# Encoder layer on one core: first norm, its products and the first weight pieces in another order

## The chip, the cores and the metric
The program runs on 1 core of one Trainium2 chip. Its engines are TensorE (PE, with its weight loads PEld), VectorE (DVE), ScalarE (ACT), GpSimd (POOL) and SyncE (SP, which here only issues transfers). The metric is the device time of one execution in microseconds (us). Three runs of the kernel before took 1007.52, 1008.33 and 1009.56 us; the median is 1008.33 us.

## The reference, cut to what matters
One post-norm layer on 512 tokens of 1024 features, all in float32. The part that the change touches is the first norm and the first products of the input projection:

```python
h = layer_norm(x, ln0_g, ln0_b)            # x: (1, 512, 1024)
proj = h @ w_in[l] + b_in[l]               # w_in: (1024, 9728)
...                                        # short convolution, dilated attention, gates
h = layer_norm(ALPHA * h + mix, ln1_g[l], ln1_b[l])
...                                        # gated MLP
h = layer_norm(ALPHA * h + ffn, ln2_g[l], ln2_b[l])
```

## The kernel before, in words
Every matrix product of float32 accuracy is made of three products of rounded operands. A weight or activation is split into a high part (`hi`, a rounded copy made on ACT) and a low part (`lo`, the rest, a subtraction); `mm3` (L312) then adds hi*hi, hi*lo and lo*hi into one PSUM tile. Here m = 0, 1, 2 names these three.

The weights come as one stream of pieces of 128 x 2048 ("chunks"; chunk 0 holds the blocks n = 0 and 1 of the input projection, chunk 1 the blocks n = 2 and 3, chunk 2 the next two). `load` (L241) issues a chunk's transfer on SP into one of only two raw buffers; `split` (L250) makes hi on ACT and lo on POOL for chunks 0 and 1, on DVE for the rest; `chunk` (L268) splits the chunk that is needed and the next, and loads the one after. A raw buffer is free once its lo is made, and the transfer of a later chunk waits on SP for that.

The first norm goes by two halves hf of two token tiles of 128 tokens (x0, x1, then x2, x3). For each half DVE computes the statistics (`bn_half`, L276), `ln_finish` (L282) makes 1/sqrt with a square root on ACT (L288) and a few tiny DVE operations, and DVE normalises x in place (L304). PE transposes x to feature-major (L345, with the identity in `cols`), ACT scales it out of PSUM (`lnT`, L308), DVE makes the high part (L309) and the low part (L310) of the eight tiles hT0 to hT7. Then PE does 96 products of 256 token columns: four blocks n, eight k, three m. The 40 bfloat16 products on `warm` (L229) at the start feed nothing. `kbd`, two tiles for the keys, are set to zero by DVE (L226).

Each engine runs its queue strictly in the order in which the instructions stand. The order is made by a scheduling layer that may move instructions of independent steps past each other; `tc.issue_after(ins)` keeps the instructions of a block that are on the engine of `ins` behind it, and `tc.keep_in_program_order` keeps marked instructions in the order of the program. The layer also decides which of the two raw buffers a new chunk gets: the one that it sees free first.

Of the kernel before, what the change touches and what calls it, by code (L numbers as in the profile page):

```python
# [11 lines left out]
P = 128  # L12
D = 1024
T = 512
KT = D // P
# [6 lines left out]
MASKED = -1e33  # L22
WARM = 40

# order of the rows of per-feature vectors that are broadcast over partitions
ROWS = ("ln0_g", "ln0_b", "b_o", "ln1_g", "ln1_b", "b_down", "ln2_g", "ln2_b")
# columns of the per-partition parameter table
C_ID = 0
# [19 lines left out]
def in_units():  # L48
    """Blocks of 128 columns of w_in in the order of their use."""
    units = []  # L50
    for p in range(NPAIR):
        for g in range(3):
            for kind, base in (("q", BLK_Q), ("k", BLK_K), ("v", BLK_V)):
                units.append((kind, p, g, base + g * 4 + p))
    for j in range(8):
        units += [("C", j, 0, BLK_C + j), ("H", j, 0, BLK_H + j), ("B", j, 0, BLK_B + j)]
    return units


def chunk_plan():  # L60
    """(name, columns) of each piece of the weight stream, in the order of its use."""
    out = [("in", i, 2048) for i in range(0, len(in_units()), 2)]
    out += [("wa", j, 2048) for j in range(0, 8, 2)]
    for j0 in (0, 4):
        out.append(("wb", j0, 2048))
        out += [("gate", j, 2048) for j in range(j0, j0 + 4)]
    for half in range(2):
        for kh in range(2):
            out.append(("wo", (half, kh), 2048))
    for part in range(2):  # L70
        for j in range(part * FFH, (part + 1) * FFH):
            out.append(("up", j, 2048))
        for half in range(2):
            for c, n in ((0, 4), (4, 4), (8, 3)):
                out.append(("dn", (part, half, c, n), n * 512))
    return out


def lay_out_weights(w):
    """The weights as one stream of [128, columns] pieces; only moves elements."""  # L80
    w_in, w_a, w_b, w_o = w["w_in"][0], w["w_a"][0], w["w_b"][0], w["w_o"][0]
# [53 lines left out]
def distance_tables():  # L135
    """-(distance) of query (partition) and key (column), MASKED where not attended to."""
    q = np.arange(P)[:, None]
# [9 lines left out]
def build(tc, x, wst, colt, dist, rows, out):  # L147
# [3 lines left out]
    with ExitStack() as ctx:  # L151
# [34 lines left out]

# [1 line left out]
        xr = x.rearrange("(i r) d -> r i d", r=4)  # L188
# [16 lines left out]

        first_load(xt[0], xr[0])
        first_load(xt[1], xr[1])
        first_raw(0, 0)
# [13 lines left out]
        nc.vector.memset(warm, 0.0)  # L222
        # keys of a pair of heads, block diagonal: rows of head h are zero outside of [:, h]
        kbd = [blk(F32R, (2, 512), f"kbd{n}") for n in range(2)]
        for t in kbd:
            nc.vector.memset(f(t), 0.0)  # L226
        wps = ps("u")
# [7 lines left out]

# [1 line left out]
        plan = chunk_plan()  # L237
# [12 lines left out]
        def split(i):  # L250
# [8 lines left out]
            for c in starts:  # L259
                part = slice(c, min(c + step, n))  # L260
                nc.scalar.activation(hi[:, part], raws[i][:, part], AF.Copy)  # L261
                eng = nc.gpsimd if i < 2 else nc.vector
                eng.tensor_tensor(lo[:, part], raws[i][:, part], f(hi[:, part]), op=ALU.subtract)  # L263
            splits[i] = (hi, lo)

        where = {(c[0], c[1]): i for i, c in enumerate(plan)}
# [7 lines left out]

# [1 line left out]
        def bn_half(st, z, h):  # L276
            nc.vector.bn_stats(out=st[:, h, :], in_=z[:, h * 512 : (h + 1) * 512])

# [3 lines left out]
        def ln_finish(sts_, name):  # L282
            n = len(sts_)
            mv = small.tile([P, 8, n], F32, tag=f"mv{n}", name=name + "mv", bufs=4)
            for i, st in enumerate(sts_):
                nc.vector.bn_aggr(out=mv[:, 0:2, i], in_=st.rearrange("p a b -> p (a b)"))
            # 1/sqrt(v): the square root's table, then one Newton step
            roots.append(nc.scalar.activation(mv[:, 2], mv[:, 1], AF.Sqrt, bias=eps).ins)  # L288
# [14 lines left out]
        def normalise(z, mean, rstd):  # L303
            nc.vector.tensor_scalar(z, z, mean, rstd, op0=ALU.subtract, op1=ALU.mult)  # L304

        def feature_major(pst, dst, kt, cg, cb, c0, c1):
            t = f32t("lnT")[:, : c1 - c0]
            nc.scalar.activation(t, pst, AF.Identity, bias=col(cb + kt), scale=col(cg + kt))  # L308
            nc.vector.tensor_copy(dst[:, 0, c0:c1], t)  # L309
            nc.vector.tensor_tensor(dst[:, 1, c0:c1], t, f(dst[:, 0, c0:c1]), op=ALU.subtract)  # L310

# [5 lines left out]
        def unit(o, w, c0, rhs, t0=0, t1=512):  # L317
            """o[128 features, tokens] = the block of weights at column c0, times rhs."""
            n = len(rhs)
# [3 lines left out]

# [1 line left out]
        stats0 = []  # L325
        hT = [blk(F32R, (2, 512), f"hT{k}") for k in range(KT)]
        first = []
        for hf in range(2):
            rr = (2 * hf, 2 * hf + 1)
            st = [bn_tile(f"l0{r}") for r in rr]  # L330
            for i, r in enumerate(rr):
                for h in range(2):
                    bn_half(st[i], xt[r], h)
            stats0 += ln_finish(st, f"l0{hf}")
            for r in rr:
                normalise(xt[r], *stats0[r])
            if hf == 0:
                with tc.issue_after(roots[0]):
                    chunk("in", 0)
            for k0 in range(0, KT, 2):  # L340
                pst = ps(("pt", "s")[k0 // 2 % 2])
                for k in (k0, k0 + 1):
# [3 lines left out]
                for k in (k0, k0 + 1):  # L346
                    c = (k % 2) * 256
                    feature_major(pst[:, c : c + 256], hT[k], k, C_G0, C_B0, hf * 256, hf * 256 + 256)
            if hf == 0:
                first = [ps("acc"), ps("acc"), ps("u"), ps("u")]  # L350
            t = slice(hf * 256, hf * 256 + 256)
            for n0, nk in ((0, [(n, k) for k in range(KT) for n in range(2)]), (2, [(n, k) for n in range(2) for k in range(KT)])):
                w = chunk("in", n0)
                for n, k in nk:
                    a = slice(n * 1024 + k * P, n * 1024 + (k + 1) * P)
                    mm3(first[n0 + n][:, t], w[0][:, a], w[1][:, a], hT[k][:, 0, t], hT[k][:, 1, t], k == 0, k == KT - 1)

# [4 lines left out]
        def nat(ap):  # L362
            """Token columns in the order (r, i) as seen in a tile whose columns are tokens 4i + r."""
            return ap.rearrange("p (i r) -> p r i", r=4)
# [3 lines left out]

# [1 line left out]
        sl = slopes()  # L370
# [42 lines left out]
        class Job:  # L413
            """Two heads times 512 columns of scores: a query tile and its window of 256 keys
            (group 0), or two residue classes of 128 queries and as many keys."""

# [68 lines left out]
            def c(self):  # L485
                """Adds to the sums over keys; rows of one head are of use in its own columns."""
                p, g, n = self.key
# [37 lines left out]
        def merge(p):  # L525
            """Weights of the groups' unnormalised outputs: exp(m_g - m) over the sum of all."""
            st1, st2 = sts[p, 1], sts[p, 2]
# [26 lines left out]

# [36 lines left out]

# [1 line left out]
        vtodo, late, scores, sums, scaled, running = [], [], [], [], [], []  # L593
# [52 lines left out]

# [1 line left out]
        ya = []  # L648
        for j in range(8):
# [55 lines left out]

# [1 line left out]
        def tok_mm(o, act, w, kts, r, k0, first, last, f0=0, f1=512):  # L707
# [28 lines left out]
        for r in range(4):  # L736
# [21 lines left out]

# [1 line left out]
        g2 = b2 = None  # L760
# [79 lines left out]
```

## Time and profile before
| What | Value |
|---|---|
| median of three runs | 1008.33 us |
| span of the profiled execution, first to last instruction | 1004.4 us |
| TensorE busy | 974.7 us, 97% of the span |
| VectorE / ScalarE / GpSimd busy | 551.0 / 398.2 / 70.2 us |
| mean granted TensorE clock | 0.985 of full speed |

The page gives no time of the profiled execution apart from its span; the 3.9 us between the span and the median of the runs lie before the first and behind the last instruction and are taken as the same for both kernels. TensorE bounds the program: after the first 15 us it hardly stops. What is read here is therefore the start, up to the last product of the first four blocks at about 41 us, and what ends each wait there.

### The profile page before, as it was taken

To read this page: it belongs to the slowest core of one execution; us is meant where nothing else is said; L and a number is where in the kernel's file an instruction comes from. 1 tells how busy PE (TensorE), PEld (TensorE's weight loads), DVE (VectorE), ACT (ScalarE), POOL (GpSimd) and SP (SyncE) were. 2 spreads that over 40 slices of the span, in tenths; PEclk is the share of its full clock that TensorE was granted. 3 is DMA by queue.
4 is the path that set the end of the run, shared out by engine and by line. 5 is a ranking of instruction groups with operands and counts; after the bars stand their busy time and mean duration, and the time that the engine had idled before them with its cause. 6 is when DMAs were issued, how large, how long until landed. Compare 5 with 4: busy or idle time off the path is not lost.

```text
span 1004.4 us, 11766 instructions
## 1 busy us (share of the span) xinstructions
PE 974.7 (97%) x4729; PEld 821.6 (82%) x4729; DVE 551.0 (55%) x863; ACT 398.2 (40%) x679; POOL 70.2 (7%) x161
## 2 busy tenths in 40 slices
PE   7999999999999999999999997799999999999996
PEld 7988888888888888888888886688888888888885
DVE  7856658657675445322355769664542345445256
ACT  4655564564543333233343223254442234444220
POOL 4000000000000000000000304400000000000000
PEclk9999999999999999999999997799999999999998
DMA  6322322122322212225243420232232322321402
GB/s 231 127 87 85 83 81 70 58 85 84 85 85 85 84 59 110 84 84 206 87 138 110 171 84 6 80 126 84 87 112 74 107 103 89 121 84 73 157 1 84
DMA packets 23462, 96.74 MB, mean 96 GB/s; under 512 B 9200, under 2 KB 9584, under 8 KB 13680
## 3 DMA queue, kind: packets, MB, share of 16 engines
q1 hardware_dynamic: 14256, 89.60, 25.6%
q0 software_dynamic: 1728, 6.29, 1.8%
q10 hardware_dynamic: 7424, 0.10, 0.4%
q8 instruction: 37, 0.61, 0.3%
q14 instruction: 17, 0.14, 0.0%
HBM read 93.84 MB, written 2.15 MB: 96 GB/s over the span
## 4 chain that ended last, share of the span: by engine, by line
PE 86%; DVE 8%; DMA 2%; ACT 2%; issue 1%; ACTq 0%; DVEq 0%
PE ps_acc L313 15%; PE ps_acc L314 15%; PE ps_acc L315 15%; PE ps_s L313 5%; PE ps_s L315 5%; PE ps_s L314 5%; PE ps_u L313 5%; PE ps_u L314 5%; PE ps_u L315 5%; PE ps_pt L313 4%; PE ps_pt L315 4%; PE ps_pt L314 4%; DMA s<-st 1%; DVE h1T L310 1%; PE ps_pt L479 1%; DVE h1T L309 1%
## 5 line engine op out<-in xcount | busy, mean ns | idle before, releaser
L263 DVE TENSOR_TENSOR lo<-raw,hi 128x1024 fp32r<-128x1024 f32 (+1 forms) x160 | 190.6, 1211 | 185.1 <-ACT hi L261 183.5
L261 ACT ACTIVATE hi<-raw 128x1024 fp32r<-128x1024 f32 (+1 forms) x166 | 166.6, 1033 | 231.0 <-PE ps_acc L314 67.5
L313 PE MATMUL ps_acc<-hT,hi 128*128 128x512 f32 (+1 forms) x512 | 198.6, 388 | 1.2 <-DVE kbd L392 0.9
L314 PE MATMUL ps_acc<-hT,hi 128*128 128x512 f32 (+1 forms) x512 | 196.7, 384 | 0.1
L315 PE MATMUL ps_acc<-hT,lo 128*128 128x512 f32 (+1 forms) x512 | 196.5, 384 | 0.0
L313 PEld LDWEIGHTS ps_acc<-hT,hi 128*128 128x128 f32 x512 | 96.5, 189 | 20.4 <-PE ps_pt L479 1.6
L315 PEld LDWEIGHTS ps_acc<-hT,lo 128*128 128x128 f32 x512 | 96.4, 188 | 19.2
L314 PEld LDWEIGHTS ps_acc<-hT,hi 128*128 128x128 f32 x512 | 96.5, 189 | 17.7 <-DVE hT L310 0.3
L460 ACT ACTIVATE S<-S,nm 128x128 f32<-128x128 f32 (+2 forms) x96 | 40.1, 419 | 54.3 <-DVE nm L458 47.5
L566 DVE SCALAR_TENSOR_TENSOR cv<-fp,cols,cv 128x512 f32<-128x512 f32 x22 | 16.5, 752 | 72.2 <-ACT cv L565 72.2
L314 PE MATMUL ps_acc<-h1T,hi 128*128 128x512 f32 (+1 forms) x96 | 38.3, 398 | 10.5 <-DVE h1T L310 5.9
L313 PE MATMUL ps_acc<-h1T,hi 128*128 128x512 f32 (+1 forms) x96 | 37.3, 389 | 3.2 <-DVE h1T L309 3.2
L315 PE MATMUL ps_acc<-h1T,lo 128*128 128x512 f32 (+1 forms) x96 | 37.1, 387 | 0.0
L314 PE MATMUL ps_s<-h1T,hi 128*128 128x512 f32 (+1 forms) x96 | 36.3, 378 | 0.0
L313 PE MATMUL ps_s<-h1T,hi 128*128 128x512 f32 (+1 forms) x96 | 36.3, 378 | 0.0
L315 PE MATMUL ps_s<-h1T,lo 128*128 128x512 f32 (+1 forms) x96 | 36.2, 377 | 0.0
L314 PE MATMUL ps_u<-h1T,hi 128*128 128x512 f32 (+1 forms) x96 | 35.7, 372 | 0.0
L315 PE MATMUL ps_pt<-h1T,lo 128*128 128x512 f32 (+1 forms) x96 | 35.7, 372 | 0.0
L314 PE MATMUL ps_pt<-h1T,hi 128*128 128x512 f32 (+1 forms) x96 | 35.7, 372 | 0.0
L313 PE MATMUL ps_u<-h1T,hi 128*128 128x512 f32 (+1 forms) x96 | 35.7, 372 | 0.0
L313 PE MATMUL ps_pt<-h1T,hi 128*128 128x512 f32 (+1 forms) x96 | 35.7, 372 | 0.0
L315 PE MATMUL ps_u<-h1T,lo 128*128 128x512 f32 (+1 forms) x96 | 35.7, 372 | 0.0
(371 smaller groups left out, 1945.7 us busy)
## 6 DMA issues: line engine op xcount, KB each, us to landing
raw<-wst SPq DMA_DIRECT2D x76, 1024.0 KB, 4.8
raw<-wst SPq DMA_DIRECT2D x4, 768.0 KB, 4.2
x<-x SPq DMA_DIRECT2D x4, 512.0 KB, 6.4
raw<-wst SPq DMA_DIRECT2D x4, 512.0 KB, 8.5
hb<-x POOLq DMA_DIRECT2D x4, 512.0 KB, 4.4
out<-hb SPq DMA_DIRECT2D x7, 256.0 KB, 2.1
ln_g<-rows POOLq DMA_DIRECT2D x3, 512.0 KB, 4.2
ln_b<-rows POOLq DMA_DIRECT2D x3, 512.0 KB, 5.4
```

The lines of the kernel that those rows point to most:

```text
L261: nc.scalar.activation(hi[:, part], raws[i][:, part], AF.Copy)
L263: eng.tensor_tensor(lo[:, part], raws[i][:, part], f(hi[:, part]), op=ALU.subtract)
L309: nc.vector.tensor_copy(dst[:, 0, c0:c1], t)
L310: nc.vector.tensor_tensor(dst[:, 1, c0:c1], t, f(dst[:, 0, c0:c1]), op=ALU.subtract)
L313: nc.tensor.matmul(o, ah, bh, start=start, stop=False)
L314: nc.tensor.matmul(o, ah, bl, start=False, stop=False)
L315: nc.tensor.matmul(o, al, bh, start=False, stop=stop)
L460: nc.scalar.activation(v, v, AF.Exp, bias=nm[:, j : j + 1], scale=0.125, accum_out=dn[:, j : j + 1])
L479: nc.tensor.transpose(pt[:, j * P : (j + 1) * P], self.pe[:, j * P : (j + 1) * P], ident)
L566: nc.vector.scalar_tensor_tensor(a, u[:, 128:640], col(c + step), a, op0=ALU.mult, op1=ALU.add)
```

## The change
x0 and x1 are loaded in two halves of 512 columns each. `kbd` is cleared on POOL. There are 56 products on `warm`. The low parts of chunk 0 are no longer made on POOL in `split`, but on DVE by the new `low`, called from the feature step of the first half: two pieces of 512 columns ahead of hT0, two ahead of hT4. The norm and the features of a half, and the products, are functions of their own. The products of the blocks 0 and 1 use the low weight parts last within each half of k. The second half's norm stands ahead of the products of the blocks 2 and 3 of the first half, its transposes ahead of those of block 3. The norm's DVE operations are pinned to program order. `chunk("in", 2)`, which splits chunk 2 and loads chunk 3, stands behind all this, with its DVE part behind the last feature operation.

```diff
-WARM = 40
+WARM = 56
...
-        first_load(xt[0], xr[0])
-        first_load(xt[1], xr[1])
+        for r in range(2):
+            for h in range(2):
+                s = slice(h * 512, h * 512 + 512)
+                first_load(xt[r][:, s], xr[r][:, s])
...
-            nc.vector.memset(f(t), 0.0)
+            nc.gpsimd.memset(f(t), 0.0)
...
-                eng = nc.gpsimd if i < 2 else nc.vector
-                eng.tensor_tensor(lo[:, part], raws[i][:, part], f(hi[:, part]), op=ALU.subtract)
+                if i > 0:
+                    low(i, hi, lo, part)
             splits[i] = (hi, lo)
+
+        def low(i, hi, lo, part):
+            eng = nc.gpsimd if i == 1 else nc.vector
+            ins = eng.tensor_tensor(lo[:, part], raws[i][:, part], f(hi[:, part]), op=ALU.subtract)
+            if i == 0:
+                pin(ins)
...
+        def first_features(hf):
+            rr = (2 * hf, 2 * hf + 1)
             for k0 in range(0, KT, 2):
+                if hf == 0 and k0 % 4 == 0:
+
+                    for n in range(2):
+                        low(0, *splits[0], slice(n * 1024 + k0 * P, n * 1024 + (k0 + 4) * P))
...
+        halves = []
+        for ks in (range(0, 4), range(4, 8)):
+            halves += [(n, k, m) for k in ks for n in range(2) for m in range(2)]
+            halves += [(n, k, 2) for k in ks for n in range(2)]
+        whole = [[(n, k, m) for k in range(KT) for m in range(3)] for n in range(4)]
+        first_norm(0)
+        with tc.issue_after(roots[0]):
+            chunk("in", 0)
+        first_features(0)
+        first = [ps("acc"), ps("acc"), ps("u"), ps("u")]
+        first_products(0, 0, halves)
+        first_norm(1)
+        first_products(0, 2, whole[2])
+        last = first_features(1)
+        first_products(0, 3, whole[3])
+        with tc.issue_after(last):
+            chunk("in", 2)
+        first_products(1, 0, [(n, k, m) for k in range(KT) for n in range(2) for m in range(3)])
+        for n in range(2, 4):
+            first_products(1, n, whole[n])
+
+        pinned[0] = False
```

In the queues this shows at three places. On SP, in the rows from the second half of raw1 on (raw1, raw2 and raw3 are the transfers of the chunks 1, 2 and 3; in brackets the semaphores that an instruction waits for), the kernel before has:

```order
L198 DMA raw1_92<-wst 128x1024
L198 DMA raw1_92<-wst 128x1024 [waits DMAHW0_49]
L198 DMA dtab_79<-dist 128x512 [waits DMAHW1_49]
L247 DMA raw2_189<-wst 128x2048 [waits DMAHW4_49,DMAHW2_49,Pool_49]
L247 DMA raw3_301<-wst 128x2048 [waits DMAHW3_49,DMAHW7_49,DMAHW0_49,Pool_49]
```

and the changed kernel has there:

```order
L198 DMA raw1_94<-wst 128x1024 [waits DMAHW1_49]
L198 DMA raw1_94<-wst 128x1024 [waits DMAHW2_49]
L198 DMA dtab_79<-dist 128x512 [waits DMAHW3_49]
L249 DMA raw2_203<-wst 128x2048 [waits DMAHW2_49,DMAHW4_49,DMAHW1_49,Pool_49]
L249 DMA raw3_437<-wst 128x2048 [waits DMAHW6_49,DMAHW5_49,DVE_49]
```

Before, raw2 waits for the transfers of raw0 (DMAHW2 and DMAHW4) and for POOL's work on it: it takes chunk 0's buffer. Now DMAHW1 and DMAHW2 are the two transfers of raw1, and the POOL work ahead of it is that on chunk 1: raw2 takes chunk 1's buffer, and raw3 takes chunk 0's, behind DVE.

On ACT, around the square root of the second half's norm (`l01mv`), the kernel before has:

```order
L308 ACTIVATE lnT_239<-ps_s_230,cols_78 128x256
L261 ACTIVATE hi1_183<-raw1_92 128x1024 [waits DMAHW7_49]
L261 ACTIVATE hi1_183<-raw1_92 128x1024 [waits DMAHW0_49]
L288 ACTIVATE l01mv_357<-l01mv_357,eps_96 128x2 [waits DVE_49]
L261 ACTIVATE hi2_295<-raw2_189 128x1024 [waits DMAHW2_49]
L261 ACTIVATE hi2_295<-raw2_189 128x1024
L308 ACTIVATE lnT_374<-ps_pt_369,cols_78 128x256 [waits PE_49]
```

and the changed kernel has there:

```order
L322 ACTIVATE lnT_257<-ps_s_248,cols_78 128x256
L263 ACTIVATE hi1_197<-raw1_94 128x1024 [waits DMAHW1_49]
L263 ACTIVATE hi1_197<-raw1_94 128x1024 [waits DMAHW2_49]
L263 ACTIVATE hi2_431<-raw2_203 128x1024 [waits DMAHW4_49]
L302 ACTIVATE l01mv_319<-l01mv_319,eps_98 128x2 [waits DVE_49]
L263 ACTIVATE hi2_431<-raw2_203 128x1024
L322 ACTIVATE lnT_360<-ps_pt_355,cols_78 128x256 [waits PE_49]
```

The first half of chunk 2's high part, which waits for raw2's transfer, has moved from behind the square root to the place just ahead of it.

On PE, the first products of block 3 and the second half's transposes (x2, x3) stand in the changed kernel as follows; before, all four blocks' products of the first half stood ahead of the first transpose of x2:

```order
L374 MATMUL ps_u_264<-hT1_166,lo1_198 128x256
L374 MATMUL ps_u_264<-hT2_167,hi1_197 128x256
L362 MATMUL ps_pt_355<-cols_78,x2_82 128x128 [waits DVE_49,PE_49]
L362 MATMUL ps_s_368<-cols_78,x2_82 128x128 [waits PE_49]
L362 MATMUL ps_pt_381<-cols_78,x2_82 128x128 [waits PE_49]
L362 MATMUL ps_s_394<-cols_78,x2_82 128x128 [waits PE_49]
L374 MATMUL ps_u_264<-hT2_167,hi1_197 128x256
L374 MATMUL ps_u_264<-hT2_167,lo1_198 128x256
L362 MATMUL ps_pt_355<-cols_78,x3_83 128x128 [waits DVE_49]
```

The transposes have moved up to the seventh product of block 3, and 17 of its 24 products stand behind the first of them.

## Rows read from the trace of the kernel before
**Rows 1.** Page, part 1: busy time, share of the span, instructions.
```profile
PE 974.7 (97%) x4729; PEld 821.6 (82%) x4729; DVE 551.0 (55%) x863; ACT 398.2 (40%) x679; POOL 70.2 (7%) x161
```
**Rows 2.** Timeline of PE, 0 to 42 us: start, length, line, operation, idle before.
```profile
1.07 6.73 PE L229 MATMUL ps_u<-warm 128*128 128x256 bf16 x40 [1.07 <-DVE warm L222]
...
15.02 0.80 PE L313 MATMUL ps_acc<-hT,hi 128*128 128x256 f32 x2
...
27.06 0.60 PE L345 MATMUL ps_pt<-cols,x 128*128 128x128 f32 x4
...
28.91 0.38 PE L313 MATMUL ps_acc<-hT,hi 128*128 128x256 f32 x1
...
29.71 0.29 PE L313 MATMUL ps_acc<-hT,hi 128*128 128x256 f32 x1
...
40.77 0.28 PE L315 MATMUL ps_u<-hT,lo 128*128 128x256 f32 x1
```
**Rows 3.** Timeline of DVE, 0 to 80 us.
```profile
9.01 3.44 DVE L304 TENSOR_SCALAR x<-x,l00mv 128x1024 f32<-128x1024 f32 x2
12.61 0.91 DVE L226 MEMSET kbd<- 128x1024 f32 x1 [0.16 <-issue]
...
18.99 1.27 DVE L277 BATCH_NORM_STATS2 l02st<-x 128x6 f32<-128x512 f32 x2
...
24.85 1.54 DVE L304 TENSOR_SCALAR x<-x,l01mv 128x1024 f32<-128x1024 f32 x2
26.30 2.35 DVE L263 TENSOR_TENSOR lo<-raw,hi 128x1024 fp32r<-128x1024 f32 x2
28.57 0.29 DVE L309 CAST hT<-lnT 128x256 fp32r<-128x256 f32 x1
...
29.23 0.49 DVE L309 CAST hT<-lnT 128x256 fp32r<-128x256 f32 x2
```
**Rows 4.** Timeline of POOL, 0 to 80 us and from 600 us.
```profile
8.96 5.85 POOL L263 TENSOR_TENSOR lo<-raw,hi 128x512 fp32r<-128x512 f32 x4 [8.53 <-ACT hi L261]
18.22 5.46 POOL L263 TENSOR_TENSOR lo<-raw,hi 128x1024 fp32r<-128x1024 f32 x2 [3.41 <-ACT hi L261]
...
607.53 2.40 POOL L756 TENSOR_TENSOR hb<-hb,ln_g 128x1024 f32<-128x1024 f32 x1 [30.49 <-PE ps_pt L733]
```
**Rows 5.** Timeline of ACT, 0 to 80 us.
```profile
7.69 0.29 ACT L288 ACTIVATE l00mv<-l00mv,eps 128x2 f32<-128x2 f32 x1 [5.47 <-DVE l00mv L286]
...
10.02 1.15 ACT L261 ACTIVATE hi<-raw 128x512 fp32r<-128x512 f32 x2 [0.62 <-DMA raw<-wst]
13.44 1.02 ACT L308 ACTIVATE lnT<-ps_pt,cols 128x256 f32<-128x256 f32 x2 [2.27 <-PE ps_pt L345]
...
17.05 2.04 ACT L261 ACTIVATE hi<-raw 128x1024 fp32r<-128x1024 f32 x2
```
**Rows 6.** Transfers of line 198 (the first loads), issue times and landing.
```profile
L198 SPq DMA_DIRECT2D raw<-wst x4: 424/506/663, 1.6 to 4.8; - x4
...
DMA to landing us min/median/max: 4.0/7.7/10.3
```
**Rows 7.** Transfers of line 247 (later chunks) up to 60 us, landing.
```profile
DMA to landing us min/median/max: 4.6/4.7/4.9
```
**Rows 8.** Timeline of DVE from 604 us: two operations beside POOL's.
```profile
607.64 5.12 DVE L310 TENSOR_TENSOR h1T<-lnT,h1T 128x256 fp32r<-128x256 f32 x2
```
**Rows 9.** Stretches with PE busy, PEld, DVE, ACT, POOL, then granted clock.
```profile
12.45:15.85 3.40, 3.35 (x15) 3.22 (x16) 3.08 (x7) 2.41 (x6) 2.37 (x2) 0.50 0.75 274
617.00:622.00 5.00, 1.77 (x7) 1.48 (x7) 5.00 (x12) 0.00 (x0) 2.75 (x2) 0.50 0.00 0
```
**Rows 10.** Timeline of PE, 613 to 627 us.
```profile
620.15 0.58 PE L314 MATMUL ps_acc<-h1T,hi 128*128 128x256 f32 x1 [4.58 <-DVE l12mv L293]
...
625.22 0.42 PE L313 MATMUL ps_s<-h1T,hi 128*128 128x256 f32 x1
...
626.50 0.41 PE L313 MATMUL ps_s<-h1T,hi 128*128 128x256 f32 x1
```

More of the change, by code (lines that the diff above doesn't have):

```diff
@@ L273, in chunk, with pin @@
             return splits[i]
+        pinned = [True]
+        def pin(ins):
+            return tc.keep_in_program_order(ins) if pinned[0] else ins
         def bn_half(st, z, h):
-            nc.vector.bn_stats(out=st[:, h, :], in_=z[:, h * 512 : (h + 1) * 512])
+            pin(nc.vector.bn_stats(out=st[:, h, :], in_=z[:, h * 512 : (h + 1) * 512]))
         def bn_tile(name):
@@ L303, in normalise @@
         def normalise(z, mean, rstd):
-            nc.vector.tensor_scalar(z, z, mean, rstd, op0=ALU.subtract, op1=ALU.mult)
+            pin(nc.vector.tensor_scalar(z, z, mean, rstd, op0=ALU.subtract, op1=ALU.mult))
         def feature_major(pst, dst, kt, cg, cb, c0, c1):
@@ L308, in feature_major @@
             nc.scalar.activation(t, pst, AF.Identity, bias=col(cb + kt), scale=col(cg + kt))
-            nc.vector.tensor_copy(dst[:, 0, c0:c1], t)
-            nc.vector.tensor_tensor(dst[:, 1, c0:c1], t, f(dst[:, 0, c0:c1]), op=ALU.subtract)
+            pin(nc.vector.tensor_copy(dst[:, 0, c0:c1], t))
+            return pin(nc.vector.tensor_tensor(dst[:, 1, c0:c1], t, f(dst[:, 0, c0:c1]), op=ALU.subtract)).ins
         def mm3(o, ah, al, bh, bl, start, stop):
@@ L326, in build, with first_norm @@
         hT = [blk(F32R, (2, 512), f"hT{k}") for k in range(KT)]
-        first = []
-        for hf in range(2):
+        def first_norm(hf):
             rr = (2 * hf, 2 * hf + 1)
@@ L333, in build @@
                     bn_half(st[i], xt[r], h)
-            stats0 += ln_finish(st, f"l0{hf}")
+            stats0.extend(ln_finish(st, f"l0{hf}"))
             for r in rr:
                 normalise(xt[r], *stats0[r])
-            if hf == 0:
-                with tc.issue_after(roots[0]):
-                    chunk("in", 0)
+        def first_features(hf):
+            rr = (2 * hf, 2 * hf + 1)
             for k0 in range(0, KT, 2):
+                if hf == 0 and k0 % 4 == 0:
+                    for n in range(2):
+                        low(0, *splits[0], slice(n * 1024 + k0 * P, n * 1024 + (k0 + 4) * P))
                 pst = ps(("pt", "s")[k0 // 2 % 2])
@@ L347, in build, with first_products @@
                     c = (k % 2) * 256
-                    feature_major(pst[:, c : c + 256], hT[k], k, C_G0, C_B0, hf * 256, hf * 256 + 256)
-            if hf == 0:
-                first = [ps("acc"), ps("acc"), ps("u"), ps("u")]
+                    last = feature_major(pst[:, c : c + 256], hT[k], k, C_G0, C_B0, hf * 256, hf * 256 + 256)
+            return last
+        def first_products(hf, n0, steps):
+            w = splits[n0 // 2]
             t = slice(hf * 256, hf * 256 + 256)
[L352 to L356, printed above, removed]
+            for n, k, m in steps:
+                a = slice(n % 2 * 1024 + k * P, n % 2 * 1024 + (k + 1) * P)
+                wk, hk = w[m // 2][:, a], hT[k][:, m % 2, t]
+                nc.tensor.matmul(first[n][:, t], wk, hk, start=k == 0 and m == 0, stop=k == KT - 1 and m == 2)
+        halves = []
[19 more added lines that the diff above has]
+        pinned[0] = False
         def evac_split(o, bias, hi, lo, src):
```

## The prediction
> **What bounds the kernel now.** I read the page's busy times first: PE is busy for 97% of the span [rows 1], so a change at the start is worth what it moves the moment from which PE runs without a stop. Then PE's timeline: 40 warm products end at 7.8, the first real product starts at 15.02, the first half's products and transposes follow closely, the second half's transposes start at 27.06, its products at 28.91, and the last product of the four blocks starts at 40.77 [rows 2]. From there on PE is fed in both kernels by the same instructions in the same order, so I compare the kernels by the time at which that last product starts. Third, the timelines of DVE, POOL and ACT show what ends each wait before it [rows 3 to 5], and the landing times what the transfers can do [rows 6, 7].
>
> **Removed, added and moved at the start.** POOL's four low parts of chunk 0 ran from 8.96 to 14.81 [rows 4], and beside them the two normalisations took 3.44 us, against 1.54 us for the second half's, beside which POOL did nothing [rows 3, 4]. Without them the first normalisation ends by 9.01 + 1.54 = 10.55 even if the halves of x bring nothing; whatever they bring is hidden, as follows. The warm products take 6.73/40 = 0.17 us each [rows 2]; 16 more at that price end by 1.07 + 6.73 + 2.7 = 10.5. Four of the 16 transposes (1.85 us for all, 27.06 to 28.91 [rows 2]) take 0.46, so PE offers the first pair by 11.0. But ACT makes the high parts of chunk 0 first: the second pair starts when its data land, at 10.02, and takes 1.15 [rows 5]. So lnT starts at about 11.2, 2.2 us earlier than 13.44, and its eight pieces, 17.05 - 13.44 = 3.6 us [rows 5], end at 14.8. DVE has meanwhile made the first two low parts, of 2.35/4 = 0.6 us each [rows 3]. The first product then starts near 11.2 + 0.9 = 12.1, 2.9 us earlier than 15.02.
>
> The two clears of kbd leave DVE (0.91 us each [rows 3]) for POOL, which has nothing to do until chunk 1. No row shows a POOL clear of this size; it could take nothing, or 2.4 us as a whole two-input operation of this size does [rows 4]. Both end long before POOL is needed at 15.9, so I take 0. If POOL's clears held DVE's clear of `warm` back, the warm products would start up to 4.8 us later and delay the first product by some 3 us, but by the next paragraphs not the end: PE waits longer than that afterwards.
>
> DVE then makes cast and rest of one tile alternately, 29.23 - 28.57 = 0.66 us per tile [rows 3]. Four tiles from 11.75 end at 14.4, two low parts of chunk 0 at 15.6, four more tiles would end at 18.2.
>
> **The chain that I expect to set the end.** It starts on ACT, behind lnT, with chunk 1. Its transfer's second half, issued at 4.8, lands 10.3 us later at 15.1 [rows 6], so ACT is the limit: two high parts of 2.04 us together [rows 5] from 14.8, the first done at 15.9. POOL makes the two low parts in 5.46 [rows 4], to 21.4. Bounds: undisturbed 2 x 2.40 = 4.8 [rows 4], and if DVE delays the second as much as it delayed the two before (5.46 - 4.8 = 0.66), 6.1. Before, the same two ran from 18.22, beside statistics on DVE; now the first meets hT4 to hT7. At 607.64 two rests on DVE took 5.12 us [rows 8] while POOL's 2.40 us operations ran. So each POOL operation can also stop DVE for some 2.4 us: hT7 is done not at 18.2 but at up to 18.2 + 4.8 = 23.0, the statistics (2 x 1.27 [rows 3], and 0.3 for the rest) at 25.8.
>
> In the changed kernel raw2 takes chunk 1's buffer, so SP issues it only at 21.4, where before it went out when POOL had finished chunk 0 (14.81). It needs 4.6 to 4.9 us [rows 7]: 26.1. On ACT the first high part of chunk 2 stands ahead of the square root of the second half's norm; it runs from 26.1 to 27.1 (half of 2.04 [rows 5]). Behind it are queued the square root, on which DVE's normalisations and PE's transposes wait, and after it every lnT of the second half. From square root to normalisation it took 9.01 - 7.69 = 1.32 [rows 3, 5]: 28.45. x2 is normalised at 29.2, x3 at 30.0 (1.54 for both [rows 3]).
>
> PE, by comparison, has its first-half products of blocks 0 and 1 done 1.3 us after hT7 (the last products with a high weight part and eight with a low one), at 24.3, block 2 (24 products of (40.77 - 29.71)/92 = 0.12 us [rows 2]) at 27.2, and the first 7 of block 3 at 28.0. So it waits for x2 until 29.2, once the square root has come. From there: 16 transposes 1.85, the 17 other products of block 3 2.04, some 0.1 for x3, and 95 steps of 0.12 to the last product, 11.4. Sum: 29.2 + 1.85 + 2.04 + 0.1 + 11.4 = 44.6, against 40.77: 3.8 us later. Included is what goes: the slow start of the second half's products (28.91 to 29.71 for three steps, 0.44 over 0.36 [rows 2]) no longer occurs, since all of block 3's rest lies between transposes and these products.
>
> **The clock.** Before, PE had 3.4 us at a granted clock of 0.50 just at the first transposes and products [rows 9]; there it had been idle from 7.8. Filled warm products and earlier transposes take that away; it is part of the 12.1 above. Now PE is short of work from about 16.5 to 23, and idle again at 28. After a wait of 4.58 us before 620.15 [rows 10] the clock was 0.50 for all of 617 to 622 [rows 9]. [...] I take 0.5, nearer to 0: most of a slow stretch would fall on products that wait for DVE or end before x2 is there.
>
> Forecast: 3.8 + 0.5 = 4.3 us. On the profiled execution that is a span of 1004.4 + 4.3 = 1008.7; with the 3.9 us outside the span, or straight on the median of 1008.33, 1012.6 us. Its own range, with POOL at 4.8 to 6.1, landing 4.6 to 4.9 and the clock at 0 to 1.2, is 3.1 to 5.8 us: 1011.4 to 1014.1.
>
> **Rivals.**
> [...]
>
> *Only DVE and POOL get in each other's way.* If raw2 lands before the square root is asked for, the norm is ready at 25.8 + 1.32 + 0.8 = 27.9 and PE does not wait at 28.0: the end moves by 3.8 - 1.2 = 2.6, 1010.9. For it: the order on ACT costs nothing then. Against: raw2 would have to land by 24.8, so to be issued by 20, and POOL's two low parts would have to be done in 4.2 us, less than 4.8.
>
> *Not slower: the early start is kept.* If neither holds, that is POOL's two operations fall into gaps of DVE, hT7 is done at 18.2 and raw2 is there when the norm asks for it, PE works from 12.1 on with some 0.6 us of waits for DVE: 2.9 + 0.4 - 0.6 = 2.7 us earlier, 1005.6. For it: PE's wait before 15.02 is the longest of the start. It decides at x2: no loss remains if x2 is normalised by 29.2 - 3.8 = 25.4, that is if raw2 lands by 22.3 and is issued by 17.5. Against: POOL's work on chunk 1, on which that issue waits, cannot begin before 15.9.
>
> **Chances.** Forecast 0.57; slow clock 0.22; DVE and POOL alone, or a wait of that order, 0.15; early start kept 0.06. A measurement of this kernel can tell some 0.2%, 2.0 us, from no change (the three runs span 2.0 us). Faster is the last rival without its edge, 0.05; within 0.2% (1006.3 to 1010.3) is the lower part of the third case and the edges of the others, 0.09; slower is the rest, 0.86. The range goes from 1010.0, which leaves out the early start and the lowest of the third case (about 0.10), to 1015.3, which leaves out slow stretches of more than 5 us (about 0.08).
>
> **What the changed profile would show.** Right: first product near 12.1 at full clock; PE gaps put down to hT on DVE from 16 to 23, with single DVE rests of some 2.4 us beside POOL's low parts; raw2 issued at about 21.4; ACT idle up to about 26 with the first high part of chunk 2 released by a transfer; the square root behind it at about 27; the first transpose of x2 near 29; the last product near 44.6 to 45. Wrong: a square root before 25, or transposes of x2 before 26, refutes the chain; a first product after 14 refutes the start; PE's last product at 44.6 with an end that differs by more than 1 us from that shift shows that something later has moved, which I hold for nothing.

## The result and the profile after

The changed kernel took 1017.82 us in the median of four runs (1016.43 to 1018.75), the kernel before 1008.2 beside it: 9.6 us slower, ratio 1.0093, 95% interval 1.0079 to 1.0108. I had forecast 1012.6 and a range up to 1015.3: the sign was right, less than half of the size.

The runs of the changed kernel come with their spans (1018.37 us with a span of 1016.6, 1016.43 with 1014.6): 1.8 us lie outside the span, not the 3.9 that I took. With the same 1.8 us its profiled execution of before was one of about 1006.2 us, 2 us quicker than its median.

The busy line shows the result at its coarsest, against [rows 1]: 8 us more of TensorE.

```profile
PE 982.6 (97%) x4745; PEld 827.5 (81%) x4745; DVE 553.6 (54%) x865; ACT 398.1 (39%) x679; POOL 66.2 (7%) x159
```

**The start.** The timeline of PE of the changed kernel, 0 to 49 us, against [rows 2]:

```profile
10.52 0.86 PE L362 MATMUL ps_pt<-cols,x 128*128 128x128 f32 x4 [1.37 <-DMA cols<-colt]
...
13.67 3.07 PE L374 MATMUL ps_acc<-hT,hi 128*128 128x256 f32 x16 [0.98 <-DVE hT L323]
...
20.35 0.38 PE L374 MATMUL ps_acc<-hT,hi 128*128 128x256 f32 x1 [1.75 <-DVE hT L323]
22.83 2.71 PE L374 MATMUL ps_acc<-hT,hi 128*128 128x256 f32 x11 [2.10 <-DVE hT L324]
...
31.48 0.27 PE L362 MATMUL ps_pt<-cols,x 128*128 128x128 f32 x1
...
46.66 0.28 PE L374 MATMUL ps_u<-hT,lo 128*128 128x256 f32 x1
```

The first product comes 1.35 us earlier than before (13.67 against 15.02), not 2.9; then PE waits twice for hT; the first transpose of x2 (31.48) carries no wait; the last product of the four blocks is at 46.66, 5.9 us later than before's 40.77. All readings by the microsecond in this document are of one profiled execution per run. What stands behind the two waits is on DVE and POOL. The timelines of DVE and of POOL, against [rows 3, 4]:

```profile
17.18 0.29 DVE L323 CAST hT<-lnT 128x256 fp32r<-128x256 f32 x1
...
17.84 2.45 DVE L323 CAST hT<-lnT 128x256 fp32r<-128x256 f32 x1
20.33 2.45 DVE L324 TENSOR_TENSOR hT<-lnT,hT 128x256 fp32r<-128x256 f32 x1
...
29.53 1.53 DVE L318 TENSOR_SCALAR x<-x,l01mv 128x1024 f32<-128x1024 f32 x2
```
```profile
0.72 1.84 POOL L228 MEMSET kbd<- 128x1024 f32 x2 [0.29 <-POOLq L875]
17.51 4.98 POOL L270 TENSOR_TENSOR lo<-raw,hi 128x1024 fp32r<-128x1024 f32 x2 [14.95 <-ACT hi L263]
```

The fifth tile's cast takes 0.29 us, the sixth's cast and rest 2.45 each, just while POOL's two operations run (17.51 to 22.49). The timeline of ACT, against [rows 5], shows the root behind the first high part of chunk 2, as forecast (28.22; I had 27.1):

```profile
11.69 1.15 ACT L263 ACTIVATE hi<-raw 128x512 fp32r<-128x512 f32 x2 [0.63 <-DMA raw<-wst]
...
27.26 1.06 ACT L263 ACTIVATE hi<-raw 128x1024 fp32r<-128x1024 f32 x1 [8.88 <-DMA raw<-wst]
28.22 0.28 ACT L302 ACTIVATE l01mv<-l01mv,eps 128x2 f32<-128x2 f32 x1
```

And a table by stretches of the changed kernel (PE, PEld, DVE, ACT and POOL busy, then the granted clock, the DMA share and GB/s) shows PE at a granted clock of 0.50 from its second wait on:

```profile
21.90:28.60 6.70, 5.77 (x27) 5.77 (x28) 5.00 (x13) 1.34 (x3) 1.02 (x3) 0.50 0.76 282
```

**The second loss, near 260 us.** From 46.66 on the two kernels run the same instructions in the same order, and up to 259 us the changed one stays 5.0 to 5.9 us late (5.7 at 259.13 against 253.42 below). Then ACT issues `s<-st` of the fourth pair of heads, 8 KB in pieces of 8 bytes through DRAM, and `st<-s` behind it on the same queue waits for it. The timeline of ACT, first of before, then of the changed kernel:

```profile
253.42 0.62 ACTq L529 DMA_DIRECT2D s<-st  x1
258.94 0.34 ACTq L533 DMA_DIRECT2D st<-s  x1
259.32 0.63 ACT L521 ACTIVATE cb<-cm 128x512 fp32r<-128x512 f32 x1 [5.93 <-DMA s<-st]
```
```profile
259.13 0.61 ACTq L571 DMA_DIRECT2D s<-st  x1
268.28 0.33 ACTq L575 DMA_DIRECT2D st<-s  x1
268.66 0.63 ACT L563 ACTIVATE cb<-cm 128x512 fp32r<-128x512 f32 x1 [9.55 <-DMA s<-st]
```

ACT stands for 9.55 us instead of 5.93; PE uses up its queued work, waits twice for about 1 us (PE's timeline) and then has the clock at 0.50 (by stretches):

```profile
269.83 0.38 PE L327 MATMUL ps_u<-PT,v 128*128 128x256 f32 x1 [1.03 <-ACT PT L523]
271.26 0.58 PE L328 MATMUL ps_u<-PT,v 128*128 128x256 f32 x1 [1.05 <-DVE PT L524]
```
```profile
271.10:277.80 6.70, 5.97 (x18) 4.83 (x19) 4.90 (x11) 6.10 (x20) 0.00 (x0) 0.50 0.00 0
```

In before neither of these two waits stands there. How much is lost here shows at a row that both kernels have in common further on, PE's row at 620.15 in [rows 10]. It is 11.2 us late in the changed kernel; in the second profile of the same kernel (c_after, below) it is 7.8 us late:

```profile
631.37 0.58 PE L328 MATMUL ps_acc<-h1T,hi 128*128 128x256 f32 x1 [4.58 <-DVE l12mv L307]
```
```profile
627.96 0.58 PE L328 MATMUL ps_acc<-h1T,hi 128*128 128x256 f32 x1 [4.58 <-DVE l12mv L307]
```

So 5.7 of the 11.2 us were there at the issue of `s<-st`, and 5.5 come from here. The spans end 12.2 us apart (1016.6 against 1004.4); the last 1.0 us arises behind 620 us and was not followed up.

The transfers in the two microseconds after each issue (queue, kind: packets, MB, share; then median us to landing), before and after:

```profile
q10 hardware_dynamic: 1040, 0.01, 23.9%
...
s<-st ACTq DMA_DIRECT2D x1, 8.0 KB, 5.5
```
```profile
q10 hardware_dynamic: 1020, 0.01, 23.8%
q8 instruction: 1, 0.02, 2.9%
...
s<-st ACTq DMA_DIRECT2D x1, 8.0 KB, 9.1
```

q10 is ACT's queue. In before all 1040 small packets have started by then; in the changed kernel 20 of them have not, and there is one packet more, of kind "instruction". The page counts them over the span:

```profile
q8 instruction: 37, 0.61, 0.2%
```

0.61 MB over 37 packets is 16 KB each; PE has 4745 products and 4745 weight loads, 9490 / 37 = 256 each. In before, the stretches from 50 to 250, 250 to 450, 450 to 600 and 640 to 840 us have 8, 8, 5 and 7 of these packets beside 2011, 1937, 1327 and 1769 products and weight loads, 242 to 265 each; of VectorE's operations there are 15 to 32 to a packet. From these counts I take the packets for PE's own instructions; no row names the engine that a packet is for. The change puts 16 warm products and their 16 weight loads ahead of everything; by the same count the packets then go out 32 PE instructions earlier in the program.

### The profile page after: what moved, and what is told of

The parts are those of the page before. It is cut to its first block, busy times and chain, and to the rows that moved or that the text cites. A ratio compares the mean times of both kernels' runs of the same rounds, so it can differ in the third digit from the quotient of the medians.

```text
span 1016.6 us, 11800 instructions
## 1 busy us (share of the span) xinstructions
PE 982.6 (97%) x4745; PEld 827.5 (81%) x4745; DVE 553.6 (54%) x865; ACT 398.1 (39%) x679; POOL 66.2 (7%) x159
## 4 chain that ended last, share of the span: by engine, by line
PE 89%; DVE 6%; DMA 2%; ACT 1%; issue 0%; SPq 0%; ACTq 0%; DVEq 0%
PE ps_acc L327 15%; PE ps_acc L328 15%; PE ps_acc L329 15%; PE ps_s L328 5%; PE ps_s L329 5%; PE ps_s L327 5%; PE ps_u L328 4%; PE ps_u L329 4%; PE ps_u L327 4%; PE ps_pt L327 4%; PE ps_pt L328 4%; PE ps_pt L329 4%; DMA s<-st 2%; DVE h1T L324 1%; PE ps_u L374 1%; PE ps_pt L521 1%
## 5 line engine op out<-in xcount | busy, mean ns | idle before, releaser
L270 DVE TENSOR_TENSOR lo<-raw,hi 128x1024 fp32r<-128x1024 f32 (+1 forms) x164 | 193.2, 1198 | 186.1 <-ACT hi L263 184.6
L327 PE MATMUL ps_acc<-hT,hi 128*128 128x512 f32 x480 | 189.8, 396 | 1.2 <-DVE kbd L434 0.9
L328 PE MATMUL ps_acc<-hT,hi 128*128 128x512 f32 x480 | 187.9, 391 | 0.0
L329 PE MATMUL ps_acc<-hT,lo 128*128 128x512 f32 x480 | 187.8, 391 | 0.0
L327 PEld LDWEIGHTS ps_acc<-hT,hi 128*128 128x128 f32 x480 | 90.6, 189 | 20.3 <-PE ps_pt L521 1.8
L329 PEld LDWEIGHTS ps_acc<-hT,lo 128*128 128x128 f32 x480 | 90.5, 189 | 19.5
L328 PEld LDWEIGHTS ps_acc<-hT,hi 128*128 128x128 f32 x480 | 90.6, 189 | 17.6
```

The lines of the kernel that those rows point to most:

```text
L270: ins = eng.tensor_tensor(lo[:, part], raws[i][:, part], f(hi[:, part]), op=ALU.subtract)
L327: nc.tensor.matmul(o, ah, bh, start=start, stop=False)
L328: nc.tensor.matmul(o, ah, bl, start=False, stop=False)
L329: nc.tensor.matmul(o, al, bh, start=False, stop=stop)
```

## The experiments

Each row shows the last product of the first four blocks (us), the packets of kind instruction in the two microseconds after the issue of the fourth `s<-st`, what that transfer took, the median, and the ratio to runs of before beside it.

| Run | warm products | last product | packets | `s<-st` | median | ratio, interval |
|---|---|---|---|---|---|---|
| before | 40 | 40.77 | 0 | 5.5 | 1008.2 | |
| c_before | 40 | 40.78 | 0 | 5.6 | 1006.46 (one run) | |
| before56 | 56 | 43.70 | 1 | 9.4 | 1013.73 | 1.0052 [1.0036, 1.0069] |
| after | 56 | 46.66 | 1 | 9.1 | 1017.82 | 1.0093 [1.0079, 1.0108] |
| c_after | 56 | 46.41 | 1 | 8.2 | 1016.95 | 1.0085 [1.0060, 1.0109] |
| after40 | 40 | 47.14 | 0 | 5.2 | 1012.03 | 1.0039 [1.0026, 1.0053] |
| xwhole | 56 | 44.35 | 1 | 9.7 | 1015.22 | 1.0070 [1.0046, 1.0094] |
| root | 56 | 46.80 | 1 | 9.1 | 1016.76 | 1.0082 [1.0058, 1.0106] |
| lo1dve | 56 | 40.62 | 1 | 9.5 | 1012.57 | 1.0051 [1.0037, 1.0065] |
| all3 | 56 | 39.85 | 1 | 8.8 | 1011.24 | 1.0032 [1.0021, 1.0042] |
| all3_40 | 40 | 40.14 | 0 | 5.5 | 1005.89 | 0.9981 [0.9969, 0.9992] |
| all3_48 | 48 | 39.98 | 0 | 5.5 | 1005.36 | 0.9974 [0.9963, 0.9985] |
| all3_40w | 40, wider | 39.46 | 0 | 5.3 | 1005.47 | 0.9969 [0.9956, 0.9982] |
| raw3_40 | 40 | 47.24 | 0 | 4.9 | 1026.52 (one run) | read at the start only, see there |

**The changed kernel again (c_after).** No edit.

> The changed kernel once more, for a second execution to read. Start theory: its last product of the first four blocks stands near 46.7 us again (40.8 before), since everything up to there hangs on fixed durations. Of the later loss (the score statistics' transfer of the fourth pair of heads, issued near 259 us, took 9.1 us instead of 5.5, and TensorE then fell to half clock): theory 'position' says that it comes again, 8 us or more and a total near 1017.5; rival 'chance of one execution' says that this transfer takes 5 to 6 us here and that the time is near 1014.

Start and second loss both came again (46.41; 8.2 us): "position", not chance. But the clock stayed at full behind it this time (1.00 from 258.5 to 290), and the second loss was 2.7 us (5.1 late at 258.49, 7.8 late at 627.96) instead of 5.5. ACT's wait was only 0.9 us shorter (8.64 against 9.55), so most of the difference is the clock: the late transfer and the lower clock behind it are two parts of that loss. The profiled execution had a span of 1011.8.

**x0 and x1 loaded whole (xwhole).**

```diff
-        for r in range(2):
-            for h in range(2):
-                s = slice(h * 512, h * 512 + 512)
-                first_load(xt[r][:, s], xr[r][:, s])
+        for r in range(2):
+            first_load(xt[r], xr[r])
```

> Changed kernel with x0 and x1 loaded whole, two transfers fewer in front. Theory A (the landings of everything behind x are late by the two extra transfers, and the whole chain to the second half's norm hangs on them): raw0, cols, x2, x3 and raw1 land 1.6 us earlier, the first product starts at 12.1 instead of 13.7, raw2 is issued near 21.0, and the last product of the first four blocks starts at 45.0 instead of 46.7: time 1.6 us lower, about 1016.2. Rival B (TensorE at half clock is what is late): the first product moves, but the last one stays within 0.5 us of 46.7.

The timelines of ACT and of PE of this run, against 11.69, 13.67 and 46.66 above:

```profile
7.74 0.30 ACT L302 ACTIVATE l00mv<-l00mv,eps 128x2 f32<-128x2 f32 x1 [5.52 <-DVE l00mv L300]
...
10.27 1.16 ACT L263 ACTIVATE hi<-raw 128x512 fp32r<-128x512 f32 x2 [0.65 <-DMA raw<-wst]
```
```profile
12.26 1.51 PE L374 MATMUL ps_acc<-hT,hi 128*128 128x256 f32 x6
...
44.35 0.28 PE L374 MATMUL ps_u<-hT,lo 128*128 128x256 f32 x1
```

Theory A holds for the landings: chunk 0's second half is there 1.4 us earlier, and so is the first product. The last product is 2.3 us earlier; the 0.9 us beyond the landings go with the clock, which was at 0.50 for 3.4 us here (21.4 to 24.8) and for 6.7 in the changed kernel, so rival B is not excluded for that part. The halves do not bring the first root forward either, they mostly delay it: in the eight profiles with whole tiles it stands at 7.67 to 8.05, in the six with halves at 7.92 to 9.85. The changed kernel's 7.92 is the earliest of its kind (c_after has 9.49).

**The second root ahead of chunk 2's high parts (root).**

```diff
-        with tc.issue_after(last):
+        with tc.issue_after(last), tc.issue_after(roots[1]):
             chunk("in", 2)
```

> Changed kernel with the square root of the second half's norm ahead of chunk 2's first high part on ACT. My forecast's theory (TensorE waits for x2, which waits for the square root, which stands behind a transfer): root at 26.9 instead of 28.2, x2 ready at 29.0, last of the first four blocks at 45.3, time lower by 1.3 us. Rival (TensorE itself is late, from the waits for VectorE at 20 and 23 us and the half clock after them): last product within 0.3 us of 46.7, time unchanged.

The root's row on ACT, now ahead of the high parts:

```profile
27.77 0.30 ACT L302 ACTIVATE l01mv<-l01mv,eps 128x2 f32<-128x2 f32 x1 [8.42 <-DVE l01mv L300]
```

The last product does not move (46.80), and 1016.76 beside c_after's 1016.95 is no gain of 1.3 us. Taken alone this is weak: the start of this execution was 1.0 us late (ACT's high parts of chunk 1 at 17.31, not 16.34), and the intervals are wider than what is looked for. One of its six executions took 1010.41 us, the others 1015.93 to 1018.02; it has no profile, and why it was quicker is open. The rival rests on the timeline of after itself, in which PE does not wait for x2.

**Chunk 1's low parts on VectorE (lo1dve).**

```diff
-                if i > 0:
+                if i > 1:
                     low(i, hi, lo, part)
...
-            eng = nc.gpsimd if i == 1 else nc.vector
+            eng = nc.vector
...
-            if i == 0:
+            if i < 2:
                 pin(ins)
...
-        first_features(0)
+        first_features(0); [low(1, *splits[1], slice(n * 1024, n * 1024 + 1024)) for n in range(2)]
```

> Changed kernel with chunk 1's two low parts on VectorE behind the eighth feature tile, instead of on GpSimd; GpSimd has then nothing to do at the start but to clear the key tiles. Theory (the two GpSimd operations stop VectorE for some 4 us): no cast or rest of a tile takes over 0.5 us, the eighth tile is done at 19.8 instead of 24.1, low parts until 22.2, statistics until 24.7, raw2 still issued near 22.3 and the root still behind it at about 28; TensorE waits some 3 us for x2, last of the four blocks at 43.4 to 45.6 (half clock after the wait or not), time 1 to 3 us lower. Rival (VectorE is merely full, GpSimd's work only came at the same time): the 2.35 us of low parts add up on VectorE and the last product is at 46.7 or later.

DVE's timeline has the sixth tile at its usual price:

```profile
17.52 0.29 DVE L323 CAST hT<-lnT 128x256 fp32r<-128x256 f32 x1
17.84 0.42 DVE L324 TENSOR_TENSOR hT<-lnT,hT 128x256 fp32r<-128x256 f32 x1
```

The last product is at 40.62, 6.0 us earlier, more than I expected: chunk 2 now got the other raw buffer and was issued at 17.01 instead of 22.52, so the root waited for no transfer; and PE, without the two waits for hT, was at full clock from 15.9 us on. The two GpSimd operations and the late chunk 2 went at once here; the run raw3_40 parts them. With the start of this kernel as early as that of before, it was still 0.5% slower, and its fourth `s<-st` took 9.5 us: the second loss does not come from the late start.

**56 warm products in the kernel before (before56), 40 in the changed one (after40).** One number each:

```diff
-WARM = 40
+WARM = 56
```

> The kernel before with 56 instead of 40 warm products and nothing else changed. In the five profiles of kernels with 56 warm products the statistics' transfer of the fourth pair of heads (s<-st) took 8.2 to 9.7 us, and one 16 KB packet of queue q8, kind instruction, started 0.5 to 1.2 us after its issue; with 40 warm products (before) that packet started 7.9 us after the issue and the transfer took 5.5 us. Theory 'code': 32 more TensorE instructions at the start move the points at which TensorE's code is loaded, so here too the packet starts within 1.5 us of the issue, the transfer takes 8 us or more, and the time is 3 to 6 us above that of before, 1010 to 1013, with the start as before (last product of the four blocks within 1 us of 40.8). Rival 'start only' (what is late later comes from the changed start): transfer 5 to 6 us, time within 1 us of before or a little lower.

> The changed kernel with 40 instead of 56 warm products and nothing else changed. Theory 'code': the code packet falls 5 us or more behind the issue of the fourth s<-st again, which takes 5 to 6 us; the start stays late (last product of the four blocks at 45.5 to 47.5); time 3 to 6 us below that of the changed kernel, 1011 to 1014. Rival 'start only': the transfer takes 8 us or more, time 1016 to 1019; with less warm work the start may get later by another 1 us.

The kernel before again (c_before), unchanged:

> The kernel before once more, for a second execution to read. Theory 'code': code packet again 7 to 9 us after the issue of the fourth s<-st, which takes 5 to 6 us. Rival 'chance': the transfer takes 8 us or more here.

The packets in the two microseconds after the issue, in before56 and in after40:

```profile
q10 hardware_dynamic: 984, 0.01, 23.2%
q8 instruction: 1, 0.02, 4.1%
```
```profile
q10 hardware_dynamic: 1040, 0.01, 23.9%
```

Sixteen warm products alone bring the loss into the kernel before, and their absence takes it out of the changed one (1012.03 against 1017.82 and 1016.95). "Code" holds in all three as far as the number of PE instructions goes. Two points of before56 missed: its time was 1013.73, where at most 1013 was expected, and its start was not as before but 2.9 us late (43.70). Its timelines of POOL and of DVE show why the start was late:

```profile
8.58 5.39 POOL L263 TENSOR_TENSOR lo<-raw,hi 128x512 fp32r<-128x512 f32 x4 [8.15 <-ACT hi L261]
```
```profile
8.60 1.27 DVE L293 TENSOR_SCALAR l00mv<-l00mv 128x2 f32<-128x2 f32 x1
9.90 1.19 DVE L294 TENSOR_TENSOR l00mv<-l00mv 128x2 f32<-128x2 f32 x1
```

POOL began at 8.58 instead of 8.96 [rows 4], just ahead of two DVE operations on two columns. They take 0.17 and 0.16 us in before and lost 2.1 us here. The rest goes with the clock, which was at 0.50 for 6.8 us (13.8 to 20.6) instead of 3.4 [rows 9]. How often an execution of before meets the same was not measured.

In after40 the chain of my forecast does bind. ACT's and PE's timelines:

```profile
28.69 1.06 ACT L263 ACTIVATE hi<-raw 128x1024 fp32r<-128x1024 f32 x1 [10.15 <-DMA raw<-wst]
29.65 0.28 ACT L302 ACTIVATE l01mv<-l01mv,eps 128x2 f32<-128x2 f32 x1
```
```profile
31.92 0.30 PE L362 MATMUL ps_pt<-cols,x 128*128 128x128 f32 x1 [1.38 <-DVE x L318]
```

**Three raw buffers (raw3_40).** after40 with one more raw buffer, read up to 50 us only, since the two tiles fewer in `tmp` change the order of later work (its one run took 1026.52 us):

```diff
-        wraw = pool("wraw", 2)
+        wraw = pool("wraw", 3)
...
-        tmp = pool("tmp", 13)
+        tmp = pool("tmp", 11)
```

> The kernel of the run after40 with three instead of two buffers for raw chunks, so that chunk 2 needs not wait for GpSimd's low parts of chunk 1; to make room, 11 instead of 13 tiles in the pool tmp, by which the order of later work changes, so only the first 50 us are read. It takes the two halves of the loss at the start apart. Theory 'exclusion' (GpSimd's two low parts stop VectorE; the wait for chunk 2 only adds a little): cast and rest of the sixth tile take 2.4 us each again, the eighth tile is done at 23.5 to 24.5, the second root at 26.5 to 27.2 instead of behind a transfer, and the last product of the four blocks falls from 47.1 by the 1.4 us that TensorE waited for x2 in after40, to 45.4 to 46.1. Rival 'chain' (the late chunk 2 is the larger part): last product at 43.5 or earlier.

The timelines of ACT, DVE and PE:

```profile
27.36 0.29 ACT L302 ACTIVATE l01mv<-l01mv,eps 128x2 f32<-128x2 f32 x1 [5.35 <-DVE l01mv L300]
```
```profile
18.43 2.44 DVE L323 CAST hT<-lnT 128x256 fp32r<-128x256 f32 x1
```
```profile
47.24 0.28 PE L374 MATMUL ps_u<-hT,lo 128*128 128x256 f32 x1
```

Chunk 2 is early, the root comes as soon as the statistics are ready, x2 is not waited for, and the last product is as late as in after40. So the chain is not the larger part: in after40 it cost 1.4 us of 6.4. My number of 45.4 to 46.1 missed too: hT was 0.4 us later, and PE, behind the same two waits for hT, worked at a granted clock of 0.50 from 22.5 to 29.2 (in after40 only from 22.6 to 26.0), by which it again reached x2 after x2 was ready.

**A version that beats both (all3_40, all3, all3_48, all3_40w).** The edits of xwhole, root and lo1dve together, with the number of warm products varied; all3_40w makes the 40 products wider:

```diff
-        warm = const.tile([P, 256], mybir.dt.bfloat16, name="warm")
+        warm = const.tile([P, 352], mybir.dt.bfloat16, name="warm")
...
-            nc.tensor.matmul(wps[:, :256], warm[:, :128], warm, start=i == 0, stop=i == WARM - 1)
+            nc.tensor.matmul(wps[:, :352], warm[:, :128], warm, start=i == 0, stop=i == WARM - 1)
```

> The changed kernel with x0 and x1 loaded whole, chunk 1's low parts on VectorE, the second root ahead of chunk 2's high parts on ACT, and 40 warm products. Theory: the start gains the 6.0 us that the low parts on VectorE gave and most of the 2.3 us that whole loads gave: last product of the four blocks at 38.4 to 40.0 (before 40.8), no late code packet at the fourth s<-st (5 to 6 us): time 1005 to 1007, 0 to 2 us below before. Rival 'code' wrong: start as early, but the fourth transfer takes 8 us or more and the time is 1009 to 1012.

> The kernel of the run all3_40 with 56 warm products of 256 columns. Theory 'code' (the number of TensorE instructions ahead decides): code packet 0.3 to 1.3 us after the issue of the fourth s<-st, which takes 8 to 10 us, time 4 to 6 us above all3_40, 1009 to 1012, though the start is at most 1 us earlier than there (last product of the four blocks at 39.0 to 40.2). Rival 'start only': transfer 5 to 6 us, time 1005 to 1006.5.

> The kernel of the run all3_40 with 40 warm products of 352 instead of 256 columns: as long as 56 of the old ones (the last ends near 10), but no more instructions. Theory 'code': code packet 7 to 9 us after the issue of the fourth s<-st, transfer 5 to 6 us; with TensorE at full clock from the first transposes the last product of the four blocks comes at 38.8 to 39.8 instead of 40.1, time 1004.4 to 1005.8. Rival 'warm time' (what moves the later loss is how long TensorE is kept warm, not how many instructions it has had): transfer 8 us or more, time 1009 to 1012.

> The kernel of the run all3_40 with 48 warm products, so the code packet falls between the two places seen: 3 to 7 us after the issue of the fourth s<-st. Theory 'start of the transfer' (in before the transfer's 1024 packets of 8 bytes had all started within 1.9 us of the issue; a code packet costs only if it starts ahead of that): transfer 5 to 6 us, time 1004.5 to 1006.5. Rival 'any overlap costs': transfer 7 us or more, time 1007 to 1010.

all3_40 is faster than before by 0.19%, with less at the start than hoped (40.14): from 10 to 14 us the granted clock was 0.61 in the mean. all3, with 16 more warm products and a start 0.3 us earlier, is 5.4 us slower than all3_40 and has the packet in the window. all3_40w keeps PE at its warm products nearly as long (to 9.97 against 10.28 in all3) with the old number of instructions. Its PE timeline and its packets after the issue:

```profile
1.13 8.84 PE L231 MATMUL ps_u<-warm 128*128 128x352 bf16 x40 [1.13 <-DVE warm L224]
...
39.46 0.28 PE L374 MATMUL ps_u<-hT,lo 128*128 128x256 f32 x1
```
```profile
q10 hardware_dynamic: 1040, 0.01, 23.9%
```

So it is the number of instructions that decides, not the warm time. all3_48 agrees with "start of the transfer", but only weakly: its packet fell later than I had worked out, 7.2 us after the issue, so the middle of the transfer was not tried. And another transfer of the same kind speaks against that theory as it stands. Before's second `s<-st`, issued at 111.21, has a packet of kind instruction 0.8 us behind its issue, ahead of its small packets, and still took 5.3 us:

```profile
q10 hardware_dynamic: 975, 0.01, 22.5%
...
q8 instruction: 1, 0.02, 3.9%
...
s<-st ACTq DMA_DIRECT2D x1, 8.0 KB, 5.3
```

The same transfer took 5.0 to 5.6 us in the four other profiles in which it has such a packet (c_before, after40, all3_40, all3_40w). So the packet alone does not make the transfer late. The 1 MB of weights is issued 1.0 us behind the second `s<-st` (112.21) and 0.8 behind the fourth; whether that decides was not tried.

Both all3_40w and all3_48 are faster than before, by 0.31% and 0.26%; between them the runs do not decide.

## Why the prediction was wrong, step by step

- **"From there on PE is fed in both kernels by the same instructions in the same order, so I compare the kernels by the time at which that last product starts."** This is the step that failed. The order is the same, but the trace has packets of kind "instruction" beside the data, 37 of 16 KB over the span, and by the count of 256 PE instructions to a packet their place in the program had moved by 32. It costs 5.4 us between the medians of all3 and all3_40, 4.9 between c_after and after40, and I held it for nothing. That the number of instructions decides is shown; how a packet makes the fourth `s<-st` late is not. The last sign of being wrong that I had named came true in kind: the end moved by 12.2 us, the last product of the four blocks by 5.9.
- **The total without these 16 products.** after40 is 4.2 us above the runs of before beside it (1012.03 against 1007.81, interval of the ratio 1.0026 to 1.0053), beside my 4.3. That this is so close is partly luck: its last product is 6.4 us later than before's (47.14 against 40.77), and the two profiled spans lie 5.5 us apart (1009.9 against 1004.4). The start was under-priced, by the next points.
- **"Whatever they bring is hidden, as follows" (the halves of x).** Wrong: I priced what they could bring, and not what two more transfers ahead of chunk 0 cost. Chunk 0 landed later (second pair of high parts at 11.69, with whole loads at 10.27), and with it the first product came 1.4 us later. Hence lnT at 12.74 instead of 11.2 and the first product at 13.67 instead of 12.1.
- **GpSimd against VectorE.** Right in kind and size: cast and rest of one tile 2.45 us each, hT7 done at 24.1 against at most 23.0, the difference being the later landing. The DVE rows of 2.45 us, which take 0.29 and 0.42 in lo1dve, stand beside POOL operations of 2.49 each (4.98 for two), the two-column ones of 1.27 and 1.19 (before56) beside POOL's of 1.35 (5.39 for four).
- **The chain over raw2 and the root.** Each link came (raw2 issued at 22.52 against 21.4, root 28.22 against 27.1), but in the changed kernel it was not the last: PE reached x2 at 31.48, after x2 was ready (29.53 + 0.8 = 30.3).
- **The clock, 0.5 us taken.** No run shows this 0.5; it was my estimate, too small and put in the wrong place. What the profile shows in its place: PE was at 0.50 for 6.7 us from its second wait for hT on, and the products in that stretch made it 1.2 us later than x2 (31.48 against 30.3). How long that stretch is differs: 3.4 us in xwhole and after40, 6.7 in raw3_40, behind the same two waits. Where it was long, moving chunk 2 ahead (raw3_40) gained nothing. The slow clock that I gave 0.22 had the place wrong too: I looked for it behind a wait for x2, and PE did not wait there.
- **The clears on GpSimd** cost nothing that shows (0.72 to 2.5, long before POOL was needed): right.
- **The time outside the span** was taken as 3.9 us and is 1.8: the profile of before that I read was of a quick execution. The runs of before spread from 1005.7 to 1010.5 us in all; its profile is one draw from them.

The last product is 2.1 us later than the 44.6 of the sum, 1.6 later than with its 0.5 for the clock: 1.1 us are the landings (the root at 28.22 against 27.1), about as much is the clock. The larger rest of the miss is what comes with the 16 warm products.

## What to carry to other kernels

Dummy instructions were not free here, although the engine was idle: with 16 more of them a packet of kind "instruction" came 0.5 to 1.2 us behind the issue of the fourth `s<-st`, some 250 us further on, and the time was about 5 us longer (5.4 between all3 and all3_40, 4.9 between c_after and after40). So when a change adds or removes instructions, look at the packets of kind "instruction" beside each short transfer on the path, as a place to search and not yet as a proof, and lengthen the warm work by its width rather than by its count: 40 products of 352 columns ended at 9.97 with a transfer of 5.3 us, 56 of 256 at 10.28 with one of 8.8. Before a first load is cut in pieces, price the transfers behind it, which landed 1.4 us later here. And keep subtractions like these off GpSimd while VectorE is on the path: beside them a cast took 2.45 us instead of 0.29, a two-column step 1.27 instead of 0.17.

## What the runs showed of the hardware that I had not expected

- Beside the data, the view of the transfers has packets of kind "instruction", 37 of 16 KB over the span, one for every 256 of PE's 9490 products and weight loads; from that count I take them for PE's. In all seven profiles with 56 warm products a packet began 0.5 to 1.2 us behind the issue of the fourth `s<-st`, and that transfer took 8.2 to 9.7 us. In the six that were read with 40 or 48 it took 5.2 to 5.6, in raw3_40 4.9. Five second transfers with a packet as near took 5.0 to 5.6, so the packet is a part of the cause at most.
- The late packets are few: in the changed kernel 20 of 1040 had not started after 2 us. None of them started from then to 264 us either, where 17 packets of weights did. Whether they stood behind the 1 MB of weights issued 0.8 us after them is not shown; the weights' transfer was not moved.
- Beside a POOL operation begun 0.02 us ahead of it, a DVE operation on two columns lasted 1.27 us instead of 0.17 (before56 against before).
